# The last LayerNorm of a decoder layer: sharing its subtractions, scalings and state copies among VectorE, GpSimd and ScalarE

## The chip, the cores and the metric

The kernel runs on one core of a Trainium2 chip. The core has TensorE (PE), VectorE (DVE), ScalarE (ACT), GpSimd (POOL) and SyncE (SP); SP here only issues DMA transfers, which 16 DMA engines carry out. The metric is the device time of one execution in microseconds (us), the median over several executions; smaller is better.

## The reference, cut to what matters

One layer of a hybrid decoder is run for 320 tokens (256 of a prompt, 8 sequences of 8 new tokens). Two token mixers (an mLSTM and an HGRN2 recurrence) read one input projection, are merged and projected, and a feed-forward block follows. The output `y` and the recurrent states are returned. What the change touches is the end:

```
x1 = LayerNorm(alpha * x + mix)
y  = LayerNorm(alpha * x1 + relu(x1 W_up)^2 W_down)        # the last norm
LayerNorm(z) = (z - mean(z)) / sqrt(var(z) + 1e-5) * g + b  # over the 2048 channels
```

and two of the states that are returned for the prompt: `new_C_prompt` (4 heads of 256 x 512) and `new_S_prompt` (8 heads of 128 x 256).

## The kernel before, in words

Activations lie transposed: channels on the 128 partitions, tokens along the row. So `z`, the input of the last norm, is 16 tiles `self.acc[:, j, :]` of 128 x 320 in one buffer, which the profile calls `f3m`. The work is one long row of matrix products on TensorE, each weight block split in a high and a low part to hold the precision of float32; the splitting costs ScalarE and VectorE one large operation each per block. The last products are those of `W_down`, one output tile `j` at a time, and `ev_dn` (L1873) adds each to `acc`.

Nothing of the order is left to the hardware beyond each engine's own queue. A planner written in Python (`Sched`, L153) runs while the kernel is built: each piece of work is a generator, a *chain* with a priority, that yields steps such as `("dve", cost, function)`. The planner keeps an estimated clock for each engine and emits a step when its inputs are due, so the order of the instructions in each engine's queue follows from estimated costs and due times. On the chip each engine takes its queue strictly in order and waits on semaphores; a DMA that waits in SP's queue holds up every DMA behind it.

The end of the kernel, in order:

- `ln_add` and `ln_sum` (L1714, L1752) keep sums of the tiles and of their squares while the `W_down` tiles come out. When the last tile is there, `ln_final` (L1770) lets two matmuls against a block of ones form the two sums over partitions. ScalarE writes the mean M (`self.lnb[3]`) and, into T, its square; VectorE makes the variance X from the second sum in PSUM and T (L1793) and clamps it and adds epsilon (L1796); ScalarE does a logarithm and an exponential (RS = exp(-0.5 ln X)); VectorE refines RS with three dependent operations (L1799 to L1801). RS (`self.lnb[4]`) is the scale. All these are 128 x 320, because M and RS are held once for every partition.
- `y` (L1889) then walks over the 16 tiles on VectorE: subtract M (L1897), two tiles later multiply by RS (L1902). The first two subtractions stand ahead of L1793 in VectorE's queue, the other fourteen behind L1801, one subtraction and one multiplication in turn. For each multiplied tile `yb_` (L1905) lets ScalarE apply the gains and offsets (`scale=g, bias=b`), and two tiles at a time go to memory by a DMA of SP (the last two tiles each by its own).
- Meanwhile TensorE computes the states. `m_C` (L1096): GpSimd issues DMAs that fetch keys and values back (`bb<-vD`, `wh<-kD`, the last work in GpSimd's queue), eight groups of six matmuls follow, ScalarE copies each result out of PSUM (`oC`, 128 x 512), and SP stores it (`Cp`, 256 KB, eight of them). `h_S` (L1558): eight heads, a product each into one of five rotating PSUM banks, and a copy out (`oS`, 128 x 256): heads 0 to 3 by ScalarE, 4 to 7 by VectorE (L1567 to L1570); SP stores two heads at a time (`Sp`, 256 KB, four of them).

All activations of ScalarE have the line L335, all matmuls L341 and all DMAs of SP L344, since they are issued by small helpers.

Of the kernel before, what the change touches and what calls it, by code (L numbers as in the profile page):

```python
# [12 lines left out]
AF = mybir.ActivationFunctionType  # L13
ALU = mybir.AluOpType
# [6 lines left out]
TOK = 320  # L21
KT = 16
# [100 lines left out]
V_MLG, V_HGG, V_G1, V_B1, V_G2, V_B2, V_LB, V_BI, V_BF, V_END = 0, 16, 32, 48, 64, 80, 96, 112, 113, 114  # L123
# [137 lines left out]
def pe_f(n, m=128):  # L261
    return max(212.0 if m == 128 else 162.0, n * 1.66)
# [35 lines left out]
class Program:  # L298
# [726 lines left out]
    def ln_post(self, h, i, src, den, hb, parts, psum):  # L1025

        v = self.nc.vector
        sm = yield acq(self.sm)
        sm_ = sm[:parts]
        em = self.colt[0:parts, (2, 3, 5)[i], h:h + 1]  # L1030
        r, st, mv = sm_[:, 0:1], sm_[:, 1:7], sm_[:, 7:9]
        yield ("dve", 80, lambda: v.tensor_scalar(r, den, em, None, ALU.max))
        yield ("dve", 80, lambda: v.scalar_tensor_tensor(r, den, -1.0, r, ALU.mult, ALU.max))
        yield ("dve", 90, lambda: v.reciprocal(r, r))
        yield ("act", act(512, psum, 1), lambda: self.A(hb, src, scale=r))
        yield ("dve", dve(512), lambda: v.bn_stats(st, hb))
        yield ("dve", 90, lambda: v.bn_aggr(mv, st))
        yield from self.rsqrt(sm_, mv[:, 1:2])
        y = sm_[:, 10:11]
        yield ("dve", dve(512, False, 2, 2), lambda: v.tensor_scalar(hb, hb, mv[:, 0:1], y, ALU.subtract, ALU.mult))  # L1040
        yield rel(self.sm, sm)
# [516 lines left out]
    def h_S(self, h):  # L1558
        x = self.sx[h]
        t = yield ("sp", 620, lambda: self.dma(x, self.sD[h]))  # L1560
        e = Ev()
        e.t = t + 3000.0
        yield wait(e, *[m["C"] for m in self.mh])
        b = yield acq(self.mbank)
        yield ("pe", 2 * pe_f(256), lambda: [self.mm(
            b[:, 0:256], x[:, 128 * i:128 * i + 128], x[:, 256 + 256 * i:512 + 256 * i], start=i == 0, stop=i == 1) for i in range(2)])
        if h < 4:  # L1567
            yield ("act", act(256, True), lambda: self.A(self.oS[:, h, :], b[:, 0:256]))
        else:
            yield ("dve", dve(256, True), lambda: self.nc.vector.tensor_copy(self.oS[:, h, :], b[:, 0:256]))  # L1570
        yield rel(self.mbank, b)
        if h % 2:
            q = slice(h - 1, h + 1)
            yield ("sp", 620, lambda: self.dma(self.d["Sp"][q].rearrange("h p v -> p h v"), self.oS[:, q, :]))
# [195 lines left out]
    def ln_final(self, n, z):  # L1770

        v = self.nc.vector
        st = self.ln[n]
        M, RS, X, T = (self.lnb[i] for i in (3, 4, 5, 6))
        q = yield acq(self.tmp)
        t = yield ("act", act(TOK), lambda: self.A(q, z, AF.Square))
        if n:
            yield wait(st["pre"])
        else:
            S1, S2 = self.lnb[0], self.lnb[1]  # L1780
            yield ("dve", dve(TOK), lambda: v.tensor_tensor(S1, S1, z, ALU.add), (t - act(TOK) - LAT,))
            yield ("dve", dve(TOK), lambda: v.tensor_tensor(q, S2, q, ALU.add), (t,))
            st["p"] = yield acq(self.sbank, 2)
            yield wait(self.slack(1000.0))
        p1, p2 = (p[:, :TOK] for p in st["p"])
        yield ("pe", pe_f(TOK), lambda: self.mm(p1, self.ones, z if n else S1, start=n == 0, stop=True))
        yield ("pe", pe_f(TOK), lambda: self.mm(p2, self.ones, q, start=n == 0, stop=True))
        yield rel(self.tmp, q)
        yield post(st["fin"])
        t = yield ("act", act(TOK, True), lambda: self.A(M, p1, scale=1.0 / D))  # L1790
        st["m"].t = t
        yield ("act", act(TOK, True), lambda: self.A(T, p1, AF.Square, scale=1.0 / D))
        yield ("dve", dve(TOK, True), lambda: v.scalar_tensor_tensor(X, p2, 1.0 / D, T, ALU.mult, ALU.subtract))  # L1793
        for p in st["p"]:
            yield rel(self.sbank, p)
        yield ("dve", dve(TOK, mode=2), lambda: v.tensor_scalar(X, X, 0.0, EPS, ALU.max, ALU.add))  # L1796
        yield ("act", act(TOK), lambda: self.A(RS, X, AF.Ln))
        yield ("act", act(TOK), lambda: self.A(RS, RS, AF.Exp, scale=-0.5))
        yield ("dve", dve(TOK), lambda: v.scalar_tensor_tensor(X, X, -0.5, RS, ALU.mult, ALU.mult))  # L1799
        yield ("dve", dve(TOK), lambda: v.tensor_tensor(X, X, RS, ALU.mult))  # L1800
        yield ("dve", dve(TOK), lambda: v.scalar_tensor_tensor(RS, X, 1.5, RS, ALU.add, ALU.mult))  # L1801
        yield post(st["end"])
# [85 lines left out]

    def y(self):  # L1889

        v = self.nc.vector
        st = self.ln[1]
        yield wait(st["m"])
        for i in range(KT + 2):
            if i < KT:
                z = self.acc[:, i, :]
                yield ("dve", dve(TOK), lambda: v.tensor_tensor(z, z, self.lnb[3], ALU.subtract), (0.0,))  # L1897
            if i == 1:
                yield wait(st["end"])
            if i > 1:  # L1900
                z = self.acc[:, i - 2, :]
                t = yield ("dve", dve(TOK), lambda: v.tensor_tensor(z, z, self.lnb[4], ALU.mult), (0.0,))  # L1902
                self.s.spawn(self.yb_(i - 2, z), 0, t)

    def yb_(self, j, z):  # L1905
        g, b = self.vec[:, V_G2 + j:V_G2 + j + 1], self.vec[:, V_B2 + j:V_B2 + j + 1]
        yield ("act", act(TOK, False, 2), lambda: self.A(z, z, AF.Identity, scale=g, bias=b))
        if j % 2 or j == 14:
            q = slice(j if j > 13 else j - 1, j + 1)
            yield ("sp", 620, lambda: self.dma(self.d["y"][:, q, :], self.acc[:, q, :]))  # L1910


    def run(self, pool):
        self.np_o = pool.tile([128, 8], F32, name="np_o")
        ns = pool.tile([128, 64], F32, name="ns_o")
        self.nso_flat = ns
        self.ns_o = ns.rearrange("p (h c b) -> p h c b", h=4, c=2)
        n0 = pool.tile([128, 64], F32, name="n0")
        self.n0 = n0.rearrange("p (h c b) -> p h c b", h=4, c=2)
        self.got, self.met = {}, {}  # L1920
        self.wx, self.n_vx, self.n_kx = [], 0, 0
        self.vx, self.kx, self.main_end = Pool([]), Pool([]), Ev()
        self.sD = [self.dr.tile([128, 768], F32, name=f"sD{j}") for j in range(HH)]
        self.kD = [self.dr.tile([128, 2, 2, 256], F32, name=f"kD{j}") for j in range(MH)]
        rows = lambda name, n, k: [self.dr.tile([32 * NB, k], F32, name=f"{name}{j}") for j in range(n)]
        self.ksD, self.vsD = rows("ksD", HH, HK), rows("vsD", HH, HV)
        self.vD = [self.dr.tile([128, 2, 2, 512], F32, name=f"vD{j}") for j in range(MH)]
        self.ln = [dict(c=Ev(), end=Ev(), pre=Ev(), m=Ev(), fin=Ev(), s=[Ev() for _ in range(KT)]) for _ in range(2)]
        self.xq, self.xq_ev = [None] * KT, [Ev() for _ in range(KT)]
        self.acc_ev = [Ev() for _ in range(KT)]  # L1930
        self.n0_in = n0
        self.start()
        self.run_main()
# [7 lines left out]
    y=(128, KT, TOK), Cp=(MH, 128, 2, DV), n_out=(128, 72), m_out=(MH, 9), Sp=(HH, 128, HV),  # L1941
# [71 lines left out]
```

## Time and profile before

| | us |
|---|---|
| median of 3 executions (lowest, highest) | 2318.72 (2317.61, 2319.37) |
| the profiled execution, its own time | 2318.6 |
| its span, first to last record | 2316.8 |
| VectorE busy | 1381.9 |
| ScalarE busy | 1043.9 |
| GpSimd busy | 12.4 |

The rows below come from that one execution; times are counted from the start of its span. The views used are: the *chain of waits* (the work that ended last, followed back from the end, in order of time), the *timeline* of one engine (start, duration, instruction, how many merged into one row), the *groups by line* (all instructions of one line and shape, with mean duration), and *busy time by stretch* (for a stretch of time, the busy time of each engine, the TensorE clock, the busy share of the 16 DMA engines and the GB/s that they moved). In a row, `out<-in` names the buffers; `f` holds M, RS, X and T and many other things. `SPq` is the issue of a DMA by SP, not the transfer.

### The profile page before, as it was taken

What the parts mean: (1) busy time and instruction counts of PE and PEld (TensorE: products, weight loads), DVE (VectorE), ACT (ScalarE), POOL (GpSimd) and SP (SyncE); (2) the same over time, 40 slices, a digit from 0 to 9 for tenths busy, and PEclk for the clock granted to TensorE, in tenths of its full rate; (3) what the DMA queues carried; (4) which work ended last, traced back from release to release, by engine and by line L of the source; (5) the groups of instructions that cost most, each with busy time, mean ns of one, the idle gap of its engine ahead of it and who ended that gap; (6) DMA issues with size and microseconds to landing.
All of it is one profiled execution on the core that took longest, in us unless ns stands there. A gap on an engine that the chain in (4) does not pass through costs nothing.

```text
span 2316.8 us, 38967 instructions
## 1 busy us (share of the span) xinstructions
PE 2306.4 (100%) x15712; PEld 2261.3 (98%) x15712; DVE 1381.9 (60%) x2418; ACT 1043.9 (45%) x1657; POOL 12.4 (1%) x45
## 2 busy tenths in 40 slices
PE   9999999999999999999999999999999999999998
PEld 8999999999999999999999999999999999999998
DVE  6566567677777776555555767544554455445555
ACT  5444445455554565444433446523443344234434
POOL 0000000000000000000000000000000000000000
PEclk9999999999999999999999999999999999999999
DMA  6787676556556654545455644444444444444465
GB/s 213 256 280 274 243 244 229 193 202 214 199 196 205 206 197 165 183 169 176 173 174 172 223 166 141 151 148 153 146 147 154 146 149 152 146 149 151 146 227 182
DMA packets 153261, 430.89 MB, mean 186 GB/s; under 512 B 17260, under 2 KB 47220, under 8 KB 152056
## 3 DMA queue, kind: packets, MB, share of 16 engines
q1 hardware_dynamic: 151928, 422.11, 53.0%
q0 software_dynamic: 1152, 6.29, 0.8%
q8 instruction: 123, 2.02, 0.4%
q14 instruction: 58, 0.48, 0.1%
HBM read 374.29 MB, written 54.05 MB: 185 GB/s over the span
## 4 chain that ended last, share of the span: by engine, by line
PE 98%; DMA 1%; DVE 1%; ACT 0%; SPq 0%; issue 0%; DVEq 0%; ACTq 0%
PE bank L341 96%; DMA wr<-wt 1%; DMA f<-xT 0%; DVE f3m L1902 0%; DVE f3m L1897 0%; PE bank L1599 0%; PE bank L1177 0%; PE bank L937 0%; DMA f<-scr 0%; PE bank L1435 0%; SPq L344 0%; PE bank L1018 0%; PE bank L1440 0%; PE bank L1548 0%; PE bank L992 0%; ACT f L335 0%
## 5 line engine op out<-in xcount | busy, mean ns | idle before, releaser
L484 DVE TENSOR_TENSOR wl<-wr,wh 128x1024 fp32r<-128x1024 f32 x423 | 518.5, 1226 | 451.1 <-ACT wh L335 448.2
L341 PE MATMUL bank<-xh,wh 128*128 128x320 f32 (+1 forms) x2408 | 782.8, 325 | 1.1 <-ACT wh L335 1.1
L341 PE MATMUL bank<-xh,wl 128*128 128x320 f32 (+1 forms) x2408 | 747.4, 310 | 0.4 <-DVE wl L684 0.4
L341 PE MATMUL bank<-xl,wh 128*128 128x320 f32 (+1 forms) x2408 | 745.5, 310 | 0.0
L335 ACT ACTIVATE wh<-wr 128x1024 fp32r<-128x1024 f32 (+1 forms) x428 | 450.9, 1054 | 448.9 <-PE bank L341 431.1
L341 PEld LDWEIGHTS bank<-xh,wh 128*128 128x128 f32 x2408 | 454.5, 189 | 19.2 <-issue 13.9
L341 PEld LDWEIGHTS bank<-xl,wh 128*128 128x128 f32 x2408 | 455.2, 189 | 3.5
L341 PEld LDWEIGHTS bank<-xh,wl 128*128 128x128 f32 x2408 | 454.4, 189 | 0.7 <-DVE wl L684 0.7
L484 DVE TENSOR_TENSOR bb<-wr,bb 128x1024 fp32r<-128x1024 f32 x179 | 219.4, 1226 | 230.3 <-ACT bb L335 230.3
L341 PE MATMUL bank<-xh,bb 128*128 128x322 f32 x1280 | 287.2, 311 | 0.0
L341 PE MATMUL bank<-ra,bb 128*128 128x320 f32 x1264 | 283.9, 309 | 0.0
L335 ACT ACTIVATE bb<-wr 128x1024 fp32r<-128x1024 f32 x179 | 188.8, 1055 | 201.4 <-PE bank L341 191.7
L341 PE MATMUL bank<-rxb,bb 128*128 128x320 f32 x1112 | 255.1, 310 | 0.0
L341 PE MATMUL bank<-ra,wh 128*128 128x320 f32 x892 | 250.3, 309 | 0.0
L341 PEld LDWEIGHTS bank<-xh,bb 128*128 128x128 f32 x1280 | 216.0, 188 | 0.0
L341 PEld LDWEIGHTS bank<-ra,bb 128*128 128x128 f32 x1264 | 210.8, 188 | 0.2
L341 PE MATMUL bank<-xl,bb 128*128 128x322 f32 x640 | 199.0, 311 | 0.0
L341 PEld LDWEIGHTS bank<-rxb,bb 128*128 128x128 f32 x1112 | 188.6, 188 | 0.2
L341 PE MATMUL bank<-rxb,wh 128*128 128x320 f32 x596 | 184.7, 310 | 0.0
L341 PE MATMUL bank<-rxb,wl 128*128 128x320 f32 x596 | 184.2, 309 | 0.0
L335 ACT ACTIVATE f<-f,misc 128x320 f32<-128x320 f32 x210 | 118.1, 562 | 138.5 <-DVE f L1865 128.7
L341 PEld LDWEIGHTS bank<-ra,wh 128*128 128x128 f32 x892 | 161.7, 188 | 1.1 <-DVE ra L1629 0.9
(273 smaller groups left out, 2235.2 us busy)
## 6 DMA issues: line engine op xcount, KB each, us to landing
wr<-wt SPq DMA_DIRECT2D x602, 512.0 KB
rx<-C SPq DMA_DIRECT2D x34, 256.0 KB
Cs<-rx SPq DMA_DIRECT2D x34, 256.0 KB
f<-C SPq DMA_DIRECT2D x30, 256.0 KB
Cs<-f SPq DMA_DIRECT2D x30, 256.0 KB
vD<-ra SPq DMA_DIRECT2D x4, 1024.0 KB
f<-S SPq DMA_DIRECT2D x8, 512.0 KB
f3h<-S SPq DMA_DIRECT2D x8, 512.0 KB
```

The source lines that it names most:

```text
L335: return self.nc.scalar.activation(out, in_, func, **kw)
L341: self.nc.tensor.matmul(*a, **kw)
L484: self.V().tensor_tensor(lo, raw, hi.bitcast(F32), ALU.subtract)
```

## The change

`ln_final` gets one more event, `x`, posted when L1796 has been issued. `y` is rewritten:

- GpSimd subtracts M from tiles 8 to 15 (`off_pool`), in its queue one after the other, from the moment M is there.
- VectorE subtracts M from tiles 0 to 7: 0 and 1 as before, 2 to 4 when X is there, ahead of the end of the scale's chain, and 5 to 7 between the first multiplications. Then it multiplies all tiles by RS; from tile 8 on each multiplication waits for GpSimd's subtraction of that tile.
- The gains and offsets (`last`) are applied by ScalarE, but for tiles 2, 5, 8, 11 and 13 by GpSimd (one `tensor_scalar` with two per-partition operands).
- All stores of `y` are of two tiles, `store`, in order, when both tiles are done.
- The copies of the heads 2 and 3 of `h_S` move from ScalarE to VectorE (`h < 4` becomes `h < 2`).

```diff
-        if h < 4:
+        if h < 2:
             yield ("act", act(256, True), lambda: self.A(self.oS[:, h, :], b[:, 0:256]))
...
         yield ("dve", dve(TOK, mode=2), lambda: v.tensor_scalar(X, X, 0.0, EPS, ALU.max, ALU.add))
+        yield post(st["x"])
...
+        def off(j):
+            return ("dve", dve(TOK), lambda: v.tensor_tensor(zs[j], zs[j], M, ALU.subtract), (0.0,))
+
+        def off_pool():
+            for j in range(8, KT):
+                yield ("pool", 750, lambda: nc.gpsimd.tensor_tensor(zs[j], zs[j], M, ALU.subtract))
+                yield post(on[j])
+
+        def last(j):
+            z, g, b = zs[j], self.vec[:, V_G2 + j:V_G2 + j + 1], self.vec[:, V_B2 + j:V_B2 + j + 1]
+            if j in (2, 5, 8, 11, 13):
+                yield ("pool", 750, lambda: nc.gpsimd.tensor_scalar(z, z, g, b, ALU.mult, ALU.add))
+            else:
+                yield ("act", act(TOK, False, 2), lambda: self.A(z, z, AF.Identity, scale=g, bias=b))
+            yield post(done[j])
+
+        def store(q):
+            yield wait(done[2 * q], done[2 * q + 1])
+            yield ("sp", 620, lambda: self.dma(self.d["y"][:, 2 * q:2 * q + 2, :], self.acc[:, 2 * q:2 * q + 2, :]))
+
         yield wait(st["m"])
-        for i in range(KT + 2):
-            if i < KT:
-                z = self.acc[:, i, :]
-                yield ("dve", dve(TOK), lambda: v.tensor_tensor(z, z, self.lnb[3], ALU.subtract), (0.0,))
-            if i == 1:
-                yield wait(st["end"])
-            if i > 1:
-                z = self.acc[:, i - 2, :]
-                t = yield ("dve", dve(TOK), lambda: v.tensor_tensor(z, z, self.lnb[4], ALU.mult), (0.0,))
-                self.s.spawn(self.yb_(i - 2, z), 0, t)
...
+        self.s.spawn(off_pool(), 1, st["m"].t)
+        for q in range(KT // 2):
+            self.s.spawn(store(q), 1)
+        for j in range(2):
+            yield off(j)
+        yield wait(st["x"])
+        for j in range(2, 5):
+            yield off(j)
+        yield wait(st["end"])
+        for j in range(KT):
+            if j < 3:
+                yield off(5 + j)
+            if j > 7:
+                yield wait(on[j])
+            t = yield ("dve", dve(TOK), lambda: v.tensor_tensor(zs[j], zs[j], RS, ALU.mult), (on[j].t if j > 7 else 0.0,))
+            self.s.spawn(last(j), 0, t)
```

The order that the planner makes of it, engine by engine: TensorE's queue is the same as before. VectorE's: subtract 0 and 1, variance (L1793), clamp (L1796), subtract 2 and 3, first refinement (now L1800), subtract 4, second and third refinement (L1801, L1802), then subtract 5, multiply 0, subtract 6, multiply 1, subtract 7, multiply 2 to 15, and six copies `oS`. GpSimd's: behind its last DMA `bb<-vD` one new instruction of kind ISA (L1904), which reloads the engine's code library, then eight subtractions (L1904) and five scalings (L1910). ScalarE's: the fifth copy `oC` now stands ahead of the first scaling. SP's: five stores `Cp`, then `y` of tiles 0-1 and 2-3, `Cp`, `y` 4-5, `Cp`, `y` 6-7, 8-9, 10-11, `Cp`, `y` 12-13, `Sp`, `y` 14-15 and three `Sp`.

More of the change, by code (lines that the diff above doesn't have):

```diff
@@ L1889, in y @@
     def y(self):
-        v = self.nc.vector
+        v, nc = self.nc.vector, self.nc
         st = self.ln[1]
-        yield wait(st["m"])
-        for i in range(KT + 2):
-            if i < KT:
-                z = self.acc[:, i, :]
-                yield ("dve", dve(TOK), lambda: v.tensor_tensor(z, z, self.lnb[3], ALU.subtract), (0.0,))
-            if i == 1:
-                yield wait(st["end"])
-            if i > 1:
-                z = self.acc[:, i - 2, :]
-                t = yield ("dve", dve(TOK), lambda: v.tensor_tensor(z, z, self.lnb[4], ALU.mult), (0.0,))
-                self.s.spawn(self.yb_(i - 2, z), 0, t)
@@ L1905, in yb_ @@
[L1905 to L1910, printed above, removed]
+        zs = [self.acc[:, j, :] for j in range(KT)]
+        M, RS = self.lnb[3], self.lnb[4]
+        on = [Ev() for _ in range(KT)]
@@ new lines, in y @@
+        done = [Ev() for _ in range(KT)]
+        def off(j):
[11 more added lines that the diff above has]
+            yield post(done[j])
@@ L1927, in run @@
         self.vD = [self.dr.tile([128, 2, 2, 512], F32, name=f"vD{j}") for j in range(MH)]
-        self.ln = [dict(c=Ev(), end=Ev(), pre=Ev(), m=Ev(), fin=Ev(), s=[Ev() for _ in range(KT)]) for _ in range(2)]
+        self.ln = [dict(c=Ev(), x=Ev(), end=Ev(), pre=Ev(), m=Ev(), fin=Ev(), s=[Ev() for _ in range(KT)]) for _ in range(2)]
         self.xq, self.xq_ev = [None] * KT, [Ev() for _ in range(KT)]
```

## The prediction, on record before the changed kernel ran

> **What bounds the kernel now.** I read the page first, then the chain of waits over the last 25 us, then the timelines of SP, VectorE and GpSimd there, then the busy time by stretch.
>
> ```profile
> span 2316.8 us, 38967 instructions
> PE 98%; DMA 1%; DVE 1%; ACT 0%; SPq 0%; issue 0%; DVEq 0%; ACTq 0%
> ...
> 2291.85 0.71 PE bank L341 x3
> ...
> 2293.18 0.39 ACT f L335
> ...
> 2293.59 0.10 DVE f3m L1897
> ...
> 2294.92 0.34 DVE f L1796
> 2295.26 0.02 issue
> 2295.28 0.47 ACT f L335
> ...
> 2296.63 0.50 DVE f L1799
> ...
> 2297.68 0.49 DVE f L1801
> 2298.18 0.40 DVE f3m L1897
> ```
>
> TensorE carries 98% of the chain, and the change leaves its queue as it was. So all before 2292.56, where TensorE leaves the chain, stays; only the last 24 us are open. There, M is ready at 2293.57 (2293.18 + 0.39), the clamp L1796 ends at 2295.25, VectorE waits 1.38 us for ScalarE's logarithm and exponential, and RS is ready at 2298.17, where L1801 ends.
>
> The chain goes on along VectorE's 32 operations. Whether they bind is for the DMA engines to say:
>
> ```profile
> 2300.72 0.33 SPq L344 DMA_DIRECT2D y<-f3m  x1
> 2301.10 0.43 SPq L344 DMA_DIRECT2D Cp<-oC  x1
> 2302.33 0.33 SPq L344 DMA_DIRECT2D y<-f3m  x1
> ...
> 2312.16 0.96 SPq L344 DMA_DIRECT2D Sp<-oS  x2
> ```
>
> ```profile
> 2293.20 0.34 SPq L344 DMA_DIRECT2D Cp<-oC  x1
> ```
>
> ```profile
> 2293.50:2294.00 0.50, 0.50 (x4) 0.41 (x3) 0.41 (x2) 0.39 (x2) 0.00 (x0) 1.00 0.00 0
> 2294.00:2294.75 0.75, 0.75 (x5) 0.62 (x4) 0.75 (x3) 0.00 (x0) 0.00 (x0) 1.00 0.90 341
> 2301.50:2310.50 9.00, 8.59 (x40) 7.16 (x38) 9.00 (x24) 8.88 (x19) 0.00 (x0) 1.00 0.97 363
> 2310.50:2311.00 0.50, 0.00 (x0) 0.00 (x0) 0.50 (x3) 0.50 (x2) 0.00 (x0) 1.00 0.13 46
> 2311.00:2315.10 4.10, 0.00 (x0) 0.00 (x0) 0.57 (x2) 0.21 (x1) 0.00 (x0) 0.85 0.99 346
> 2315.10:2316.80 1.70, 0.00 (x0) 0.00 (x0) 0.00 (x0) 0.00 (x0) 0.00 (x0) 0.50 0.01 4
> ```
>
> The last two figures of a row are the DMA engines' busy share and GB/s. A store issued at 2293.20 moves data from 2294.00: 0.8 us after its issue. From 0.8 us behind the first store of `y` (2300.72) until 2315.1 the DMA engines are full but for half a microsecond. They move 9.00 x 363 + 0.5 x 46 + 4.10 x 346 = 4.71 MB; that is all of `y` (2.62), four `Cp` (1.05) and four `Sp` (1.05). Then 1.7 us pass to the end. So **the tail is a stream of stores**: its end is the first `y` store + 0.8 + bytes / 0.36 MB per us + idle time in the stream + 1.7. Check: 2300.72 + 0.8 + 13.1 + 0.4 + 1.7 = 2316.7, span 2316.8. VectorE matters through when it lets the stream begin and whether it starves it. The last pair of `Sp` is issued at 2312.16 while older transfers still run.
>
> **The change, part by part.**
>
> ```profile
> L484 DVE TENSOR_TENSOR wl<-wr,wh 128x1024 fp32r<-128x1024 f32 x423 | 518.5, 1226 | 451.1 <-ACT wh L335 448.2
> ```
>
> ```profile
> L1897 DVE TENSOR_TENSOR f3m<-f3m,f 128x320 f32<-128x320 f32 x14 | 6.9, 490 | 0.0
> ```
>
> ```profile
> 2310.15 1.42 DVE L1570 COPY oS<-bank 128x256 f32<-128x256 f32 x4
> ```
>
> ```profile
> 2297.59 2.88 PE L341 MATMUL bank<-bb,wl 128*128 128x512 f32 x12
> ```
>
> *VectorE.* Eight subtractions leave it. One takes 0.49 us, but in a row they start 0.40 apart (2298.18 to 2298.58 in the chain), so 3.2 us go. Two copies of `oS` come, 0.33 apart ((1.42 - 0.43) / 3 in the row above, with one copy 0.43). Subtractions 2 and 3 fit into the 1.38 us gap at no cost; subtraction 4, between two refinements that wait for each other, has 0.49 - 0.40 of its own cover and adds about 0.3 us to RS. Undisturbed, VectorE would multiply tile 15 about 4 us earlier, at 2306.
>
> *Stores.* ScalarE's fifth `oC` copy now precedes the first scaling. Its six matmuls are the first half of the twelve in the last row and end at 2299.0, so its `Cp` can issue at about 2299.6 instead of 2301.10 and use idle DMA time; 4.46 MB remain behind the first `y` store. This term helps: 0.26 MB, 0.7 us.
>
> *GpSimd.* It gets eight two-input subtractions, five scalings and a code reload. None is in the trace of before; the nearest rows:
>
> ```profile
> 0.73 0.20 POOL L620 MEMSET ones<- 128x128 f32 x1 [0.29 <-POOLq L2002]
> 0.87 0.53 POOL L638 MEMSET f<- 128x512 f32 x1
> 14.38 0.57 POOL L639 COPY f<-f 128x128 f32<-128x128 f32 x1 [12.98 <-DMA f<-wif]
> ...
> 25.55 0.40 POOL L716 CAST ra<-f 128x256 fp32r<-128x256 f32 x1 [9.46 <-DMA f<-spread]
> ```
>
> ```profile
> L1292 POOL MEMSET f<- 128x320 f32 x6 | 2.2, 368 | 623.3 <-DVE f L1290 381.3 <-PE bank L341 146.4 <-DVE misc L1052 95.6
> ```
>
> ```profile
> 13.98 0.82 DVE L684 TENSOR_TENSOR xl<-f,xh 128x640 fp32r<-128x640 f32 x1
> ...
> 15.87 0.83 DVE L684 TENSOR_TENSOR xl<-f,xh 128x640 fp32r<-128x640 f32 x1
> ```
>
> The memsets cost (0.53 - 0.20) / 384 = 0.86 ns per element over about 0.1 us fixed. If two inputs come one after the other, a subtraction of 320 takes 0.1 + 2 x 320 x 0.86 ns = 0.65, a little more for the write: I take **0.73 us**. Ends: 0.37 (the memset of 320, no input) and 1.42 (the COPY of 128 scaled to 320); 0.73 is nearer to the cast and the memsets, five rows against one. For a scaling, one input, I take 0.45 us: between the memset's 0.37 and the cast's 0.40 x 320 / 256 = 0.50.
>
> *Do the two engines block each other?* The COPY is the row to weigh. It reads 128 elements and takes 0.57 us, longer than the CAST, which reads 256 in 0.40. While the COPY ran, VectorE ran a subtraction of two SBUF operands from 13.98 to 14.80; the COPY ended 0.15 us after it. It looks held until VectorE let go. That is one row (its short rows may cost something too), but all that GpSimd gets here reads SBUF, and nearly all that VectorE does here has two SBUF operands. I forecast that they take turns. What VectorE holds is at least the part that grows with size, (1226 - 490) / 704 = 1.045 ns per element, 0.33 us for 320, and at most the pitch, 0.40; GpSimd 0.64 to 0.73.
>
> The Trainium skill, page "SBUF — State Buffer", section "Who interferes with whom", says that a VectorE instruction with two SBUF inputs contends with a GpSimd instruction that reads SBUF, and that the loser is blocked for the whole instruction, not slowed. The COPY row agrees. By that rule the sum below takes its upper end, a time of 2322.1; if the two met only for the moments in which data streams, the lower, 2320.8.
>
> *The sum.* GpSimd begins near 2293.6, when M is there. Up to RS, eight VectorE operations with two SBUF inputs (subtract 0 to 4, three refinements), the clamp and all eight subtractions of GpSimd want their turn: 8 x 0.33 + 0.33 + 8 x 0.64 = 8.1 us, or 8 x 0.40 + 0.33 + 8 x 0.73 = 9.4 us; the variance from PSUM and ScalarE's two steps lie beside it. RS is ready at 2301.7 to 2303.0 instead of 2298.17. From RS to the first `y` store passed 2.55 us; with the same four VectorE operations and no `oC` copy between the two scalings I take 2.4: 2304.1 to 2305.4, not 2300.72. The stream then ends at 2304.1 + 0.8 + 4.46 / 0.36 (12.4) + 1.7 = 2319.0, or 2320.3, so 2.2 to 3.5 us after 2316.8. I take **+3.0**, above the middle, since the reload can only delay GpSimd. With 0.37 for a subtraction RS would be ready near 2299 and the end about where it was (2318.5); with 1.42 it would be 2307 and the time near 2326. The end of VectorE, delayed by later turns to 2311 to 2313, then six copies, gives a last `Sp` issue near 2313 to 2315, which the stream still covers (it would be 2318.3 with 0.8 + 0.7 + 1.7).
>
> The profiled execution took 2318.6 and the median is 2318.72, 0.1 apart; 2318.6 + 3.0 = **2321.6 us**.
>
> **The rivals.**
>
> *No blocking: a small gain.* If the COPY was slow for its shape only, the first store leaves at 2300.75 as before (RS 0.3 later, one `oC` less between), the stream carries 4.46 MB: 2300.75 + 0.8 + 12.4 + 1.7 = 2315.65. The second store leaves near 2302.0, when tile 3 is scaled, and its data come 0.3 behind the first's: 2316.0, time 2317.8. For it: the VectorE subtraction beside the COPY took no longer (0.82) than one alone (0.83). Against: the COPY row. More is hardly to be had: 3.2 us fewer on VectorE meet a DMA stream that is full.
>
> *VectorE goes first: slower.* In the row above it was GpSimd that was held. If VectorE always wins, GpSimd gets in only in gaps, VectorE runs up to multiplication 8 at about 2302.8 and waits there for GpSimd, which has some six subtractions left (4.4 us) with eight multiplications among them (3.2 us); GpSimd scales tile 2 only when that is done, near 2310.3. The store of tiles 2-3 waits for it at the head of SP's queue, and all behind it. From its issue 4.13 MB are left: + 0.8 + 11.4 + 1.7 = + 13.9. It costs from an issue at 2302.9 on, and over 0.2% from 2307.5 on; at 2310.3 the span is 2324.2, the time 2326.0.
>
> *The code reload is late.* It stands behind the last GpSimd DMA:
>
> ```profile
> 2287.39 0.53 POOL L1100 DMA_DIRECT2D bb<-vD  x1 [6.14 <-PE bank L341]
> ```
>
> From 2287.92 to M are 5.65 us of cover. Without blocking the store of tiles 2-3 leaves at T + 8 x 0.73 + 0.45 + 0.05 where T is GpSimd's start, so a reload of 8.6 us still costs nothing against before and one of 13.3 us costs 4.6. No row bounds it. The Trainium skill, "GPSIMD Engine Reference", section "Instruction dispatch", gives about 6 us for the first call after a load; by it T is 2294 if the load starts at once, or about 2299.6 if it starts with the first call, and then the end is 3 us late even without blocking.
>
> **How the numbers follow.** A measurement of this kernel can tell about 0.2%, 4.6 us, from no change: 2314.1 to 2323.4. Turns, 0.45 (2320.5 to 2322.5; with slow GpSimd operations above 2323.4, 0.04 of it); no blocking, 0.26 (2317.8, with 0.02 for over 4.6 us faster, which no row gives); VectorE first, 0.12 (2326); late reload alone, 0.17 (2318 to 2325, 0.10 of it above 2323.4). Faster 0.02, slower 0.04 + 0.12 + 0.10 = 0.26, same 0.72. The range runs from the gain less the spread of before, 2317.3, to 2325.0; it leaves out VectorE first and the worst of the reload and of slow GpSimd operations, under 0.2 together. That the change is not carried out is no case: the order of the instructions shows all its parts.
>
> **What would show it.** Right: GpSimd's subtractions start near 1.1 us apart until RS, those of VectorE among them likewise; RS at 2301.7 to 2303.0; first `y` store at 2304.1 to 2305.4; full DMA engines from there. No blocking: RS at 2298.5 and first store at 2300.8. VectorE first: multiplications 0.40 apart up to tile 7 and a long wait of SP for GpSimd at its second `y` store. Late reload: an idle GpSimd behind 2293.6. My sum is wrong if the copies `oS`, not the stream, end last.

## The result, and the profile after

| | before | after |
|---|---|---|
| median, us (lowest, highest; executions) | 2318.55 (2317.61, 2320.32; 6) | 2326.93 (2325.6, 2329.98; 6) |
| ratio after / before, 95% interval | | 1.0036 (1.0026, 1.0046) |
| profiled execution, its own time / span, us | 2318.6 / 2316.8 | 2328.1 / 2326.3 |
| M (see below), us | 2293.59 | 2295.47 |
| from M to the end of the span, us | 23.24 | 30.86 |

The change is slower by 8.4 us. In the two profiled executions M is taken as the start of VectorE's first subtraction of the last norm, and all below is counted from it: M varied from 2292.9 to 2297.3 in the kernels of this study, whose work ahead of M is the same. Of the difference of the two spans 1.9 us lie ahead of M, and 7.6 us behind it. Only the 7.6 us are explained below; the 1.9 us are within the scatter of M.

VectorE's timeline of after (start, duration, instruction, how many merged):

```profile
2295.47 1.58 DVE L1900 TENSOR_TENSOR f3m<-f3m,f 128x320 f32<-128x320 f32 x2 [1.91 <-ACT f L335]
...
2297.89 2.25 DVE L1900 TENSOR_TENSOR f3m<-f3m,f 128x320 f32<-128x320 f32 x2
2300.06 1.17 DVE L1800 SCALAR_TENSOR_TENSOR f<-f 128x320 f32<-128x320 f32 x1
2301.15 1.17 DVE L1900 TENSOR_TENSOR f3m<-f3m,f 128x320 f32<-128x320 f32 x1
2302.24 1.16 DVE L1801 TENSOR_TENSOR f<-f 128x320 f32<-128x320 f32 x1
2303.43 1.05 DVE L1802 SCALAR_TENSOR_TENSOR f<-f 128x320 f32<-128x320 f32 x1
2304.41 0.48 DVE L1900 TENSOR_TENSOR f3m<-f3m,f 128x320 f32<-128x320 f32 x1
2304.81 0.48 DVE L1934 TENSOR_TENSOR f3m<-f3m,f 128x320 f32<-128x320 f32 x1
...
2306.41 5.70 DVE L1934 TENSOR_TENSOR f3m<-f3m,f 128x320 f32<-128x320 f32 x14
```

GpSimd's timeline, and the tile view of `f3m` for it (durations in ns: shortest, median, longest):

```profile
2295.58 8.56 POOL L1904 TENSOR_TENSOR f3m<-f3m,f 128x320 f32<-128x320 f32 x8 [5.76 <-ACT f L335]
2307.00 7.96 POOL L1910 TENSOR_SCALAR f3m<-f3m,vec 128x320 f32<-128x320 f32 x5 [2.87 <-DVE f3m L1934]
```

```profile
L1904 POOL TENSOR_TENSOR f3m<-f3m,f x8: 959/1123/1127, 2295.6 to 2303.0; 128x320 f32<-128x320 f32 x8
L1910 POOL TENSOR_SCALAR f3m<-f3m,vec x5: 597/598/5601, 2307.0 to 2314.4; 128x320 f32<-128x320 f32 x5
```

There are two phases. **Until RS** both engines go in step: while GpSimd's eight subtractions run (2295.58 to 2304.14), VectorE's operations start 1.09 apart (2300.06, 2301.15, 2302.24) and last 1.16, against 0.40 to 0.49 before. RS is ready at 2304.48, M + 9.0 instead of M + 4.6. **From RS on** VectorE runs at its undisturbed 0.40 per operation, fourteen multiplications in 5.70 us, and GpSimd's first scaling, which begins at 2307.00 by the record, lasts 5.6 us: to 2312.6, half a microsecond after the last multiplication (2312.11). The other four take 0.60.

What the stores make of it: SP's timeline, SP's waits (total, times, longest), and the busy time by stretch (PE, weight loads, VectorE, ScalarE, GpSimd, TensorE clock, then the share of the DMA engines and GB/s):

```profile
2306.80 6.16 SPq L344 DMA_DIRECT2D y<-f3m  x2
2313.01 0.42 SPq L344 DMA_DIRECT2D Cp<-oC  x1
...
2320.19 2.25 SPq L344 DMA_DIRECT2D Sp<-oS  x3
```

```profile
SPq L344 <- POOL f3m L1910: 4.9, 2, 4.6
```

```profile
2307.50:2309.00 1.50, 0.94 (x4) 0.49 (x3) 1.50 (x5) 1.50 (x4) 1.50 (x1) 1.00 0.57 218
2309.00:2313.00 4.00, 2.73 (x10) 1.79 (x11) 4.00 (x11) 4.00 (x10) 4.00 (x2) 1.00 0.00 0
...
2313.50:2324.50 11.00, 1.89 (x9) 1.33 (x7) 1.27 (x3) 0.34 (x1) 1.46 (x3) 0.74 1.01 372
2324.50:2326.30 1.80, 0.00 (x0) 0.00 (x0) 0.00 (x0) 0.00 (x0) 0.00 (x0) 0.50 0.03 8
```

The first row of SP merges two issues: the first at 2306.80 (M + 11.33; before M + 7.13), the second, 0.33 ahead of the row's end, at 2312.63 (M + 17.16; before M + 8.74). That store, tiles 2 and 3, waits for GpSimd's scaling of tile 2, and everything behind it in SP's queue waits with it: the DMA engines move the first store and then nothing from 2309 to 2313. From the second store's issue the rule that the prediction states for a late second store, + 13.9, gives 2326.5, and the span is 2326.3.

### The profile page after: what moved, and what is told of

Its sections match the earlier page's. It is cut to its first block, busy times and chain, and to the rows that moved or that the text cites. A ratio compares the mean times of both kernels' runs of the same rounds, so it can differ in the third digit from the quotient of the medians.

```text
span 2326.3 us, 38974 instructions
## 1 busy us (share of the span) xinstructions
PE 2308.6 (99%) x15712; PEld 2261.4 (97%) x15712; DVE 1384.1 (59%) x2412; ACT 1040.9 (45%) x1650; POOL 30.1 (1%) x58
## 4 chain that ended last, share of the span: by engine, by line
PE 96%; DMA 1%; DVE 1%; ACT 0%; issue 0%; SPq 0%; ACTq 0%; DVEq 0%
PE bank L341 95%; DMA wr<-wt 1%; PE bank L1599 0%; PE bank L1177 0%; PE bank L937 0%; DMA f<-scr 0%; DVE f3m L1900 0%; DVE bb L484 0%; ACT f3m L335 0%; PE bank L1435 0%; ACT bb L335 0%; DVE wl L484 0%; SPq L344 0%; ACT wh L335 0%; PE bank L1018 0%
## 5 line engine op out<-in xcount | busy, mean ns | idle before, releaser
L341 PEld LDWEIGHTS bank<-xh,wh 128*128 128x128 f32 x2408 | 454.0, 189 | 20.0 <-issue 13.9
```

What stands on the lines that cost most here:

```text
L341: self.nc.tensor.matmul(*a, **kw)
```

## The experiments

M, the first and the second `y` store and the end are taken from one profile of each kernel, "held" is GpSimd's longest scaling (in pool_mul its one multiplication). Each ratio is to executions of before taken together with that kernel, whose medians lie between 2318.48 and 2319.36, so it isn't the quotient of two numbers of this table. Kernels with one execution have no ratio.

| kernel | median, us (executions) | ratio to before, 95% | held, us | 1st, 2nd `y` store, M + | M to end |
|---|---|---|---|---|---|
| before | 2318.55 (6) | | | 7.13, 8.74 | 23.2 |
| after | 2326.93 (6) | 1.0036 (1.0026, 1.0046) | 5.6 | 11.33, 17.16 | 30.9 |
| psum | 2318.71 (10) | 0.9997 (0.9987, 1.0006) | 0.61 | 8.33, 9.56 | 23.2 |
| warm_scale | 2327.47 (5) | 1.0035 (1.0022, 1.0048) | 5.6 | 11.34, 17.17 | 30.9 |
| subs_only | 2324.43 (10) | 1.0022 (1.0013, 1.0032) | none | 11.35, 12.92 | 29.4 |
| rest_only | 2318.6 (10) | 0.9998 (0.9989, 1.0007) | none | 7.27, 8.84 | 22.8 |
| scales_only | 2324.57 (8) | 1.0027 (1.0017, 1.0038) | 8.8 | 7.27, 16.24 | 29.2 |
| psum_rs | 2319.78 (10) | 1.0006 (0.9997, 1.0015) | 0.61 | 9.90, 11.14 | 24.8 |
| psum_m | 2320.42 (10) | 1.0006 (0.9997, 1.0016) | 1.5 | 9.56, 11.20 | 24.9 |
| pool_mul | 2321.27 (10) | 1.0009 (1.0, 1.0018) | 4.2 | 7.27, 8.84 | 25.3 |
| early_mul | 2319.41 (11) | 1.0002 (0.9993, 1.0011) | none | 7.14, 8.23 | 23.8 |
| tiny_two | 2327.24 (1) | | 5.6 | 11.35, 17.25 | 30.9 |
| tiny_one | 2327.75 (1) | | 5.6 | 11.36, 17.27 | 31.0 |
| break7 | 2326.06 (10) | 1.0028 (1.0019, 1.0038) | 1.5 | 11.36, 13.00 | 26.7 |
| mid_psum | 2322.78 (10) | 1.0014 (1.0005, 1.0024) | 1.6 | 11.35, 13.16 | 26.9 |
| mid_sbuf | 2327.59 (5) | 1.0037 (1.0023, 1.0052) | 6.0 | 11.34, 17.57 | 31.3 |
| mid_psum2 | 2323.29 (1) | | 1.6 | 11.35, 13.16 | 26.9 |

Two theories were there for the 5.6 us. **T**: the two engines exclude each other when VectorE reads two operands from SBUF and GpSimd reads SBUF, in turns or one holding the other out. **F**: the first call of another kind of GpSimd operation pays for the loading of its code.

### psum: VectorE takes M and RS from PSUM

```diff
-            return ("dve", dve(TOK), lambda: v.tensor_tensor(zs[j], zs[j], M, ALU.subtract), (0.0,))
+            return ("dve", dve(TOK), lambda: v.scalar_tensor_tensor(zs[j], p1, -1.0 / D, zs[j], ALU.mult, ALU.add), (0.0,))
...
+        Q = p2 if n else RS
-        yield ("act", act(TOK), lambda: self.A(RS, RS, AF.Exp, scale=-0.5))
+        yield ("act", act(TOK), lambda: self.A(Q, RS, AF.Exp, scale=-0.5))
```

The three refinements and the multiplications use `Q` and `p2` in place of RS, and the two PSUM banks are kept. GpSimd's work is that of after.

> VectorE takes the mean and the scale of the last norm from PSUM, so that each of its operations there has one operand in SBUF; GpSimd's work stays. From M to the end of the span passed 23.2 us before and 30.9 us in the changed kernel. Theory T (turns: VectorE operations with two SBUF operands and GpSimd operations that read SBUF shut each other out, and a run of VectorE multiplications keeps GpSimd's first scaling out until it ends): VectorE's operations start 0.40 us apart, GpSimd's subtractions take about 0.75, the scale is ready 4.9 us behind M, the first scaling by GpSimd takes 0.6, and M to the end is about 22.5 us, some 2318 us in all. Rival F (first call: the first scaling on GpSimd pays about 5 us to load its code, whoever holds SBUF): the subtractions are freed as well, but the first scaling still takes 5.6 us and the second store of y leaves 13.3 us behind M; M to the end about 27 us, 2322.5 us in all.

The tile view for GpSimd and two rows of VectorE:

```profile
L1906 POOL TENSOR_TENSOR f3m<-f3m,f x8: 869/873/959, 2293.1 to 2299.0; 128x320 f32<-128x320 f32 x8
L1912 POOL TENSOR_SCALAR f3m<-f3m,vec x5: 605/608/608, 2301.5 to 2305.9; 128x320 f32<-128x320 f32 x5
```

```profile
2294.90 0.94 DVE L1797 TENSOR_SCALAR f<-f 128x320 f32<-128x320 f32 x1
...
2300.91 5.65 DVE L1937 TENSOR_TENSOR f3m<-f3m,bank 128x320 f32<-128x320 f32 x14
```

The same thirteen GpSimd operations now take 0.87 and 0.61 us each, beside a VectorE that runs at 0.40: no turns, no scaling held, and the whole loss is gone. That speaks for T and against F, since the scaling is called for the first time here too. What remains blocked is the clamp, with 0.94 us instead of 0.33. The Trainium skill, page "SBUF — State Buffer", section "Who interferes with whom", says that a VectorE operation with at most one SBUF input does not contend with GpSimd outside the two-port modes, and that `tensor_scalar` can enter such a mode. Both halves agree with these rows.

### warm_scale: the scaling's code called early

```diff
+        g0, b0 = self.vec[:, V_G2:V_G2 + 1], self.vec[:, V_B2:V_B2 + 1]
+        yield ("pool", 200, lambda: nc.gpsimd.tensor_scalar(self.warm, self.warm, g0, b0, ALU.mult, ALU.add))
         yield wait(st["m"])
```

`warm` is a buffer of its own, 128x8.

> The changed kernel with one more GpSimd scaling, of an unused 128x8 tile, right behind the code reload and before M is there. Theory T: nothing changes for the stores; the first real scaling still takes about 5.6 us and ends about 0.5 us behind VectorE's last multiplication; M to the end 30.9 us, as in the changed kernel. Rival F: the small scaling takes about 5 us in GpSimd's idle time, the first real scaling 0.6 to 1.2 us, the second store leaves some 4.5 us earlier and M to the end is about 26.5 us, 2322.5 us in all.

```profile
2291.14 0.54 POOL L1100 DMA_DIRECT2D bb<-vD  x1 [6.15 <-PE bank L341]
2291.80 0.35 POOL L1920 TENSOR_SCALAR warm<-warm,vec 128x8 f32<-128x8 f32 x1
2297.44 8.56 POOL L1904 TENSOR_TENSOR f3m<-f3m,f 128x320 f32<-128x320 f32 x8 [5.29 <-issue]
```

```profile
L1910 POOL TENSOR_SCALAR f3m<-f3m,vec x5: 600/601/5602, 2308.9 to 2316.2; 128x320 f32<-128x320 f32 x5
```

The first real scaling still takes 5602 ns: F is refuted.

### subs_only, rest_only, scales_only: the change in halves

```diff
-            if j in (2, 5, 8, 11, 13):
+            if j in ():
```

is subs_only (GpSimd subtracts, ScalarE scales all tiles). scales_only leaves that line alone and drops GpSimd's subtractions; rest_only does both, so GpSimd does nothing:

```diff
-        self.s.spawn(off_pool(), 1, st["m"].t)
...
-            if j < 3:
+            if j < 11:
                 yield off(5 + j)
-            if j > 7:
-                yield wait(on[j])
```

> The changed kernel with all sixteen scalings on ScalarE; GpSimd keeps its eight subtractions. Both theories: the scale is ready 9.0 us behind M as in the changed kernel, the first store of y leaves 11.4 us behind M, the second store no longer waits for GpSimd, and the stream of stores ends 11.4 + 0.8 + 12.4 + 1.7 = 26.3 us behind M: about 3 us over before, 2321.7 us in all. If M to the end stays near 30.9 us, the stores were not held by the scalings.

> The rest of the change without GpSimd: VectorE subtracts from all tiles (three subtractions in and behind the gap), ScalarE scales all, two copies of heads move to VectorE, stores in pairs. Both theories: the scale is ready 4.9 us behind M, no VectorE operation takes over 0.5 us, and M to the end is 22.6 to 23.4 us, within 0.6 us of before; 2318 to 2319 us in all. If it is over 25 us, part of the loss came from the order of the work and not from GpSimd.

> VectorE subtracts from all tiles, GpSimd has the five scalings alone. The scale is ready 4.9 us behind M as before. Theory S: VectorE's operations follow one another without a gap until about 15.6 us behind M, the first scaling becomes ready 7.6 us behind M and takes some 8 us, the second store of y leaves 15.8 us behind M, and M to the end is 15.8 + 13.9 = 29.7 us: 6.5 us over before, 2325 us in all, nearly the whole loss of the change although the scale is on time. Rival: if the late scale was what cost, M to the end is 23 us, 2319 us in all.

rest_only came out as expected: all that does not concern GpSimd is worth nothing to the time. scales_only:

```profile
L1910 POOL TENSOR_SCALAR f3m<-f3m,vec x5: 602/604/8755, 2301.0 to 2311.6; 128x320 f32<-128x320 f32 x5
```

```profile
2300.85 0.33 SPq L344 DMA_DIRECT2D y<-f3m  x1
2301.34 0.33 SPq L344 DMA_DIRECT2D Cp<-oC  x1
2309.82 0.33 SPq L344 DMA_DIRECT2D y<-f3m  x1
```

With RS and the first store on time, five scalings of 0.6 us alone cost 6.0 us, against 7.6 for the whole change, because the first is held for 8.8.

subs_only missed its expectation of 26.3 by 3.1 us, and not on GpSimd's account: its first store left at M + 11.35, as in after, and the second 1.6 later. ScalarE's timeline shows what came out of the planner for sixteen scalings, and TensorE's waits (total, times, longest) what that did:

```profile
2304.42 0.58 ACT L335 ACTIVATE oC<-bank 128x512 f32<-128x512 f32 x1
2304.90 7.73 ACT L335 ACTIVATE f3m<-f3m,vec 128x320 f32<-128x320 f32 x14
2312.53 1.06 ACT L335 ACTIVATE oC<-bank 128x512 f32<-128x512 f32 x2
```

```profile
PE bank L341 <- DVE oS L1570: 4.6, 2, 4.1
```

Fourteen scalings stand in one row ahead of the last two `oC` copies, the PSUM banks stay full, TensorE waits, and the last `Sp` is late. The row of waits names VectorE's `oS` since the bank that came free first was the one that VectorE copies out behind its multiplications (at 2309.78); the other four were left to ScalarE, whose copies began at 2312.53. So this run does not price the subtractions by themselves; psum_rs and mid_psum below come nearer to it.

### psum_rs and psum_m: one operand each

Each is a part of psum: only RS, or only M, comes from PSUM.

> Only the scale RS goes to PSUM for VectorE; the mean stays in SBUF. The queues of GpSimd and ScalarE are those of the changed kernel. Theory T: the subtractions still take turns, but the refinement of the scale and the multiplications have one SBUF operand and let GpSimd in; the first scaling by GpSimd takes 0.6 us. The scale is ready some 7.5 us behind M (three refinements freed of the nine that took turns), the first store leaves about 9.9 us behind M and the rest follows as a stream: M to the end 9.9 + 0.8 + 12.4 + 1.7 = 24.8 us, 2320.2 us in all. If the first scaling still takes over 5 us, the multiplications are not what holds it.

> Only the mean goes to PSUM for VectorE; the scale stays in SBUF. The queues of GpSimd and ScalarE are those of the changed kernel. Theory T: VectorE's subtractions run at 0.40, the three refinements take turns with GpSimd, the scale is ready some 7.5 us behind M and VectorE's multiplications end about 15 us behind it; GpSimd's first scaling waits for that end, the second store of y leaves about 15.6 us behind M, and M to the end is 15.6 + 13.9 = 29.5 us, 2325 us in all. If the loss of the changed kernel came mostly from the late scale, M to the end would be about 25 us.

psum_rs came out as expected, 24.8: the multiplications leave GpSimd alone, its scalings take 0.61, and only the late scale is paid for. psum_m was expected at 29.5 and gave 24.9. Its multiplications read two SBUF operands as those of after do:

```profile
L1911 POOL TENSOR_SCALAR f3m<-f3m,vec x5: 836/1464/1475, 2304.2 to 2310.0; 128x320 f32<-128x320 f32 x5
```

```profile
2303.66 6.71 DVE L1936 TENSOR_TENSOR f3m<-f3m,f 128x320 f32<-128x320 f32 x14
```

Yet GpSimd got in, one scaling per 1.46 us, and VectorE's fourteen multiplications took 6.71 instead of 5.70, 0.25 for each of the four scalings that it let by. T names the two parties but not who wins.

### pool_mul: is it the kind of operation?

Two answers: **K**, a scaling loses where a `tensor_tensor` takes turns; **S**, a GpSimd operation that comes into a running row of two-operand VectorE operations is held until the row ends. Here VectorE does all subtractions and all multiplications but that of tile 13, which is GpSimd's only operation, and ScalarE all scalings:

```diff
+            if j == 13:
+                continue
...
+            t = yield ("pool", 750, lambda: nc.gpsimd.tensor_tensor(zs[j], zs[j], RS, ALU.mult))
```

> VectorE subtracts from all tiles, ScalarE scales all, and GpSimd has one operation, the multiplication of tile 13 by RS (two SBUF inputs), which becomes ready in the middle of VectorE's row of operations with seven of them still to come behind its subtraction. Theory S (a streak of VectorE operations with two SBUF operands that follow one another without a gap keeps out a GpSimd operation that comes later): the one operation takes about 3 to 4 us and ends 0.5 to 0.9 us behind VectorE's last multiplication; VectorE's stay 0.40 apart. Rival K (it is the kind: GpSimd's tensor_scalar gets no turn, its tensor_tensor does): it takes at most 1.2 us, and one VectorE operation takes 1.1 us instead of 0.49. M to the end 22.8 to 23.5 us by both, 2319 us in all.

```profile
2305.41 4.20 POOL L1908 TENSOR_TENSOR f3m<-f3m,f 128x320 f32<-128x320 f32 x1 [17.49 <-DVE f3m L1900]
```

```profile
2306.80 2.09 DVE L1937 TENSOR_TENSOR f3m<-f3m,f 128x320 f32<-128x320 f32 x5
```

```profile
2309.64 3.38 ACT L335 ACTIVATE f3m<-f3m,vec 128x320 f32<-128x320 f32 x6 [2.46 <-POOL f3m L1908]
```

The operation that takes 1.1 in turns was held 4.20 us, to 0.7 behind VectorE's last multiplication (2308.89): K is refuted. The end, 25.3 instead of at most 23.5, was not foreseen: five scalings of ScalarE stood in its queue behind that of tile 13.

### early_mul: an attempt at a faster kernel

Without GpSimd, the first five tiles, which VectorE has subtracted by then, are multiplied right behind the scale.

```diff
+            if j > 4:
+                yield off(j)
+            t = yield ("dve", dve(TOK), lambda: v.tensor_tensor(zs[j], zs[j], RS, ALU.mult), (0.0,))
```

> No work on GpSimd; VectorE subtracts from tiles 0 to 4 ahead of the scale and multiplies these five right behind it, before it goes on with the other subtractions. By the picture of the tail as a stream of stores that begins with the first store of y: the first store leaves 0.8 us earlier than with the rest of the change alone (6.5 us behind M instead of 7.3), and M to the end is about 22.0 us instead of 22.8 and 23.2 before: some 1 us under before, 0.05%, which the times of whole executions will hardly tell. If M to the end stays at 22.8, the stream is not set by its first store.

The first store stayed at M + 7.14 and the end came at 23.8 instead of 22.0: ScalarE's queue has an `oC` copy between the scalings of tiles 0 and 1, so an earlier multiplication of tile 1 bought nothing. That explains the first store, not the end. The end is late since from tile 5 on each multiplication stands right behind the subtraction of its own tile and has to wait for its result: such a pair takes 0.93 (multiplications start at 2301.15 and 2302.08), where rest_only, whose pairs are of two different tiles, takes 0.81 (2301.08 and 2301.89). VectorE's last multiplication ends 17.2 us behind M instead of 15.7, and the last stores of `y` leave later.

```profile
2299.14 0.66 ACT L335 ACTIVATE f3m<-f3m,vec 128x320 f32<-128x320 f32 x1 [0.63 <-DVE f3m L1931]
2299.70 0.58 ACT L335 ACTIVATE oC<-bank 128x512 f32<-128x512 f32 x1
2300.18 2.83 ACT L335 ACTIVATE f3m<-f3m,vec 128x320 f32<-128x320 f32 x5
```

### tiny_two, tiny_one, break7: what breaks the row?

The first two add to after an operation of 128x8 ahead of the third multiplication (`src` is `w[:, 0:8]` or the PSUM bank); the last lets only subtraction 7, which stands there, take M from PSUM. Where a PSUM bank is read, it is kept to the end.

```diff
+                yield ("dve", dve(8), lambda: v.scalar_tensor_tensor(w[:, 0:8], src, -1.0 / D, w[:, 0:8], ALU.mult, ALU.add), (0.0,))
```

```diff
+            if j == 7:
+                return ("dve", dve(TOK), lambda: v.scalar_tensor_tensor(zs[j], st["p"][0][:, :TOK], -1.0 / D, zs[j], ALU.mult, ALU.add), (0.0,))
```

> The changed kernel with one more VectorE operation of 128x8 on an unused tile between subtraction 7 and multiplication 2; both its operands lie in SBUF. Theory S (an unbroken streak of two-operand operations keeps GpSimd out, and an operation with one SBUF operand breaks the streak): the streak stays whole, and GpSimd's first scaling takes 5.5 us and ends half a us behind the last multiplication. Rival P (phase: GpSimd gets in or not by how its attempts fall against VectorE's 0.40 us period, and any shift can change it): the first scaling takes about 1.4 us, as with the mean in PSUM.

> The same extra VectorE operation at the same place, but with its first operand from PSUM, so that it has one operand in SBUF. Theory S: the streak starts anew behind it and GpSimd gets in: its five scalings take about 1.4 us each, the second store of y leaves some 4 us earlier than in the changed kernel, and M to the end is about 27 us instead of 30.9. Rival P: it does the same as the extra operation with both operands in SBUF, whichever way that goes.

> The changed kernel with the mean of tile 7 alone taken from PSUM: the VectorE operation just ahead of multiplication 2 has one operand in SBUF. No instruction is added. Theory S: GpSimd's scalings take about 1.4 us each, the second store leaves 12.9 us behind M instead of 17.1, and M to the end is 26.3 to 27 us, about 2322.5 us in all. Rival P, or any theory in which the multiplications alone decide: the first scaling still takes 5.6 us and M to the end is 30.9 us.

The tile view of tiny_one, then that of break7:

```profile
L1911 POOL TENSOR_SCALAR f3m<-f3m,vec x5: 602/604/5607, 2306.6 to 2314.0; 128x320 f32<-128x320 f32 x5
```

```profile
L1913 POOL TENSOR_SCALAR f3m<-f3m,vec x5: 834/1462/1473, 2306.6 to 2312.4; 128x320 f32<-128x320 f32 x5
```

In tiny_one a short operation with one SBUF operand (0.15 us) freed nothing, and in tiny_two the 0.08 us by which both shift VectorE's work changed nothing either; each is one execution. In break7's profile the scalings took 834 to 1473 ns and the end came at 26.7, as S said. But its ten executions fall into two groups, 2321.1 to 2323.6 (four, the profiled one among them) and 2325.8 to 2328.5 (six); the second lies where after lies. So a full-width operation half a microsecond before GpSimd asks seems to let it in on some executions only. This is read from the times, since none of the slower six has a profile. And where the outcome varies from one execution to the next, the single executions of tiny_one and tiny_two settle neither S nor the rival of phase.

### mid_psum, mid_sbuf, mid_psum2: a gap while GpSimd waits

After, with one more full-width VectorE operation between the multiplications 5 and 6 (its result is read by nobody); `src` is the PSUM bank in mid_psum, M in mid_sbuf, and mid_psum2 has three of them.

```diff
+            for _ in range(1 if j in (6,) else 0):
+                w = self.lnb[5]
+                yield ("dve", dve(TOK), lambda: v.scalar_tensor_tensor(w, src, -1.0 / D, w, ALU.mult, ALU.add), (0.0,))
```

> The changed kernel, with one more VectorE operation of full width (128x320, one operand from PSUM, one from SBUF, result in a buffer that nobody reads) between the multiplications 5 and 6, when GpSimd's first scaling has been waiting for over 1 us. Theory S (a waiting GpSimd operation gets in at the next VectorE operation that has only one SBUF operand): the first scaling ends at this operation and takes 1.3 to 2.2 us instead of 5.6; the second y store goes out at M + 13 to 14 instead of M + 17.16. Rival P (whether GpSimd gets in is settled when it asks, at the beginning of VectorE's run of operations, and one gap later doesn't free it): the first scaling takes about 6.1 us, its old 5.6 and the added operation, and M to the end is about 31.3.

> The control of the run beside it: the added operation of full width between the multiplications 5 and 6 has two SBUF operands. S and P both expect a first scaling of about 6.0 us (5.6 + 0.4) and M to the end of 31.0 to 31.5. If it is short here too, it is not the operand that matters but where VectorE's work stands.

> As the first of these runs, with three such operations in a row between the multiplications 5 and 6, so that VectorE leaves at least 1.2 us. S: the first scaling ends there, 1.3 to 2.6 us long; the second scaling, ready by then, follows in the same gap with about 0.6 us. P: 5.6 + 3 x 0.4 to 0.5, about 7 us.

mid_psum, VectorE's timeline, then the tile view for GpSimd:

```profile
2303.89 1.68 DVE L1938 TENSOR_TENSOR f3m<-f3m,f 128x320 f32<-128x320 f32 x4
2305.50 0.48 DVE L1935 SCALAR_TENSOR_TENSOR f<-bank,f 128x320 f32<-128x320 f32 x1
2305.90 4.87 DVE L1938 TENSOR_TENSOR f3m<-f3m,f 128x320 f32<-128x320 f32 x10
```

```profile
L1911 POOL TENSOR_SCALAR f3m<-f3m,vec x5: 837/1473/1582, 2304.5 to 2310.4; 128x320 f32<-128x320 f32 x5
```

mid_sbuf, the same two views:

```profile
2306.05 0.47 DVE L1935 SCALAR_TENSOR_TENSOR f<-f 128x320 f32<-128x320 f32 x1
2306.45 4.09 DVE L1938 TENSOR_TENSOR f3m<-f3m,f 128x320 f32<-128x320 f32 x10
```

```profile
L1911 POOL TENSOR_SCALAR f3m<-f3m,vec x5: 597/598/6006, 2305.0 to 2312.8; 128x320 f32<-128x320 f32 x5
```

S foretold this pair rightly: the waiting scaling is let in at the operation with one SBUF operand and lasts 1.6 us at the longest instead of 6.0, and from there on the scalings keep getting turns (ten multiplications in 4.87, not 4.09). Whether this one operation takes an operand from PSUM or from SBUF is worth 4.8 us by the medians (2327.59 and 2322.78; five and ten executions that don't overlap), 4.4 from M to the end. Rival P of these three runs, that the matter is settled when GpSimd asks, is refuted.

S is not the whole of it, as psum_m has shown, where the first scaling came into a running row and was let in. mid_psum2 shows the same: there the third scaling asks at 2310.05, in the midst of a running row, and has its turn after 1.4 us:

```profile
2308.67 4.60 DVE L1938 TENSOR_TENSOR f3m<-f3m,f 128x320 f32<-128x320 f32 x10
```

```profile
2310.05 3.71 POOL L1911 TENSOR_SCALAR f3m<-f3m,vec 128x320 f32<-128x320 f32 x3 [1.67 <-DVE f3m L1938]
```

In every kernel here, once a scaling had been let in against a row of two-operand multiplications, the later ones were too. What puts the two engines into one mode or the other at first (turns among the subtractions, held out among the multiplications, either in break7) stays open.

## Why the prediction was wrong, step by step

- *All before M stays; the end is a stream of stores.* Right, as far as the scatter of M (4.4 us between kernels) lets the first half be seen. From the second `y` store's issue the predicted + 13.9 gives M + 31.1 for after, 25.1 for psum_m, 27.1 for mid_psum and 31.5 for mid_sbuf, against 30.9, 24.9, 26.9 and 31.3. The rule needs that nothing starves the stream later: in subs_only, pool_mul and early_mul the end came 1.7 to 2.6 us behind it, and in scales_only 0.9 ahead of it.
- *The engines take turns, so RS comes at M + 8.1 to 9.4 and the first store at M + 10.5 to 11.8.* Right: M + 9.0 and M + 11.33. psum shows that it is the SBUF operands. There is some luck in the size: a subtraction takes 0.87 us alone (psum) where I took 0.73. With 0.87, or 0.77 without the 0.1 that I took as fixed, the same sum gives 9.1 to 10.5 us instead of 8.1 to 9.4, and the measured 9.0 lies just under its low end. A pair of turns took 1.09, near 0.33 + 0.77.
- *The sum: + 3.0 us.* **This step failed**, in that it let the stream begin at the first store and run without a hole: the rule has a term for idle time in the stream, and the sum put it at nothing. With the first store at M + 11.33 the sum gives M + 26.2; the end came at 30.86, so the term was 4.6 us. Behind RS the prediction charged the turns to VectorE alone (its end at 2311 to 2313) and set a scaling of GpSimd at 0.45 us, though it meets the same multiplications and the second store waits for it. Alone a scaling takes 0.60; the first was held 5.6, the second store went out 5.83 us behind the first (1.61 in before), and the DMA engines stood still (0.00 from 2309 to 2313). Where the scalings do get in, with all else as in after, the step is nearly right: mid_psum takes 3.6 us longer than before from M to the end, and its median is 2322.78, 3.4 over that of before on the same chip, where I forecast + 3.0 and 2321.6. The rest, 30.86 - 26.88 = 4.0 us, is the scaling held out.
- *The rival "VectorE goes first"*, 2326.0 with a chance of 0.12, had the right price (2326.93) and half of the mechanism: SP's second `y` store did wait for the scaling of tile 2 until VectorE's row ended. But VectorE did not go first before RS, and never waited at multiplication 8. I set "turns" and "VectorE first" against each other as two worlds; the two followed one another within 12 us, and I found nothing in the trace of before that could order them. The range, which ended at 2325.0, left this rival out.
- *Losses don't add up.* The late scale, with scalings that take turns, is worth 3.6 us (mid_psum), the held scaling alone 6.0 (scales_only), both together 7.6. In scales_only as in after the second store leaves half a microsecond behind the end of VectorE's row, at M + 16.24 and M + 17.16, though RS came at M + 4.9 in the one and M + 9.0 in the other.
- *The code reload.* No cost: GpSimd began 0.11 us after M, behind 5.76 us of idle time. The Trainium skill, page "GPSIMD Engine Reference", section "Instruction dispatch", gives about 6 us for the first call after a load. No run here shows such a time. In warm_scale the record of the first call stands 0.66 us behind that of the last DMA and is 0.35 us long, and whatever the load took was over 5.6 us later, when the subtractions began on time.
- *Fewer operations on VectorE, the `oC` copy ahead, the copies `oS`.* Worth next to nothing: rest_only, which has all of them, takes 22.8 us from M to the end against 23.24, where the case without blocking was forecast 0.8 us faster than before, and its times, at 0.9998 (0.9989 to 1.0007), can't show either. None of the kernels here is measurably faster than before.

## What to carry to other kernels

Before work goes to GpSimd beside VectorE, count what VectorE reads from SBUF in that stretch: with two SBUF operands, each GpSimd operation here cost a turn of both engines at best (1.09 us a pair in after) and waited for the end of VectorE's row at worst (5.6 us). With one of VectorE's operands kept in PSUM, both ran at full speed (psum). And ask of a queue in order, here SP's, which single result stands at its head: one 0.6 us operation held up 4 MB of stores.

## What the hardware showed that was not expected

- Blocking is not one for one. The Trainium skill, page "SBUF — State Buffer", section "Summary: rules for kernel authors", has the second to issue blocked until the first finishes. Here a scaling that came during multiplication 3 waited until multiplication 15 was over (5.6 us) and in scales_only longer (8.8), while in other kernels a waiting operation got its turn after two or three (1.46 us).
- One VectorE operation with a PSUM operand in the midst of a row released GpSimd (6.0 to 1.6 us); a 0.15 us one, half a microsecond ahead of GpSimd's request, did not in its one execution (tiny_one).
- The same program seems to go either way from one execution to the next: break7 has times at 2321 to 2324 and at 2326 to 2328, of which only the first group has a profile.
